# A decoder layer on one core: late weight blocks are loaded only after the last raw load of their projection

## The chip, the cores and the metric

The kernel runs on one core of one Trainium2 chip. The metric is the device time of one execution in microseconds; lower is better.

## The reference

One layer of a hybrid decoder over 256 positions of width 2048, in float32: a gated feed-forward network (FFN) at half weight, a mixer of attention and mLSTM heads behind one input projection and before one output projection, a second FFN, and a last norm.

```python
x = x + 0.5 * swiglu(rmsnorm(x, ffn1_norm), w_gate1, w_up1, w_down1)   # 2048 -> 5632 -> 2048
h = rmsnorm(x, mix_norm)
parts = split(h @ w_in)                                                # 2048 -> 6152
y = concat(diff_attention(...), mlstm(...))
x = x + y @ w_out                                                      # 2048 -> 2048
x = x + 0.5 * swiglu(rmsnorm(x, ffn2_norm), w_gate2, w_up2, w_down2)
out = rmsnorm(x, final_norm)
```

Nearly all of the work is in the projections (`@`). Each weight is used once, so all weights stream from HBM through the core: the profile counts 349.56 MB read.

## The kernel before, in words

**Splitting.** A float32 product is made of three matmuls in a faster format: each operand is split into a high and a low half (`split_weights`, L117 and L118 by way of `split`: ACT casts the high half `wh`, DVE subtracts it to make the low half `wl`), and `mms` (L166, L167, L169) adds high x high, low x high and high x low in PSUM. The pool `wsp` holds four pairs of `wh` and `wl`; ACT can only split the next weights when PE has used the oldest pair.

**Paired projections.** Two column blocks of 512 columns, from the weights `wa` and `wb` (gate and up of an FFN, or two neighbouring blocks), are computed together by the class `Paired`. For the first `ns` pairs of rows tiles (128 rows each) it uses a scheme with seven products instead of eight for a 2 x 2 block of weights (as Strassen's and Winograd's): sums of weight blocks take the place of a product. The other rows (`rest`) are multiplied plainly (`plain`, loads of `rawp` at L204). `ns` is 5 for most projections, 3 or 2 for the down projections and for a few of the mixer.

**The four blocks of a pair.** `load` (L430 and, through `load_pair`, L193) brings three of them into a tile `raw`: slot 0 is the first row tile of `wa`, slots 1 and 2 are both row tiles of `wb`. The fourth, the second row tile of `wa`, is called the late block. `late` (L495) loads late blocks two at a time into a tile `late` of the pool `wrp`, which has five buffers and serves the `rawp` tiles too. The `raw` tiles are in the pool `wr` with six buffers; a projection with `ns` = 5 takes five of them, so one is free for the projection that follows.

**Order within a projection.** `leading` loads the raw tiles, splits slot 0, and adds blocks on DVE (L463). `second_sum` then splits slot 0 again and adds slot 2 to it, with an accumulating DMA (L479, `raw<-raw`) where `ns` is over 3, or else on DVE. `sums` loads the late blocks, splits slot 0 once more (`part` with S2), adds the late blocks to slot 0 with accumulating DMAs (L517, `raw<-late`), multiplies the late blocks bare (`bare`), and goes on with slot 1. `second` uses slots 0 and 2, and frees the raw tiles. `Chain.run` runs the leading part of a projection between the last steps of the one before.

**Queues.** A scheduler orders each engine's instructions by their place in the program and by priorities; loads are moved forward by 400 places (`AHEAD`). SP's queue carries the `rawp` and `late` loads of all projections. The raw loads go on POOL's queue (`nc.gpsimd`), with the accumulating DMAs, except in the first chains of both FFNs (`ON_POOL` = 3), where they go on SP's too. A queue issues in order: where one issue waits, all behind it on that engine wait.

Of the kernel before, what the change touches and what calls it, by code (L numbers as in the profile page):

```python
# [42 lines left out]
LK = 4  # L43
# [17 lines left out]
def tile_trunk_layer(ctx: ExitStack, tc: tile.TileContext, x, xt, par, bias_if, lamv, fnorm,  # L61
                     wg1, wu1, wd1, wqk0, wqk1, wqk2, win, wout, wg2, wu2, wd2, out):
    nc = tc.nc
# [14 lines left out]
    def nm(s):  # L78
        uid[0] += 1
        return f"{s}_{uid[0]}"  # L80
# [43 lines left out]
    def after(late, early):  # L124

        tc.add_manual_dep(late.ins, early.ins.name,
                          mybir.DependencyInfo(mybir.DependencyClass.NoSync, mybir.DependencyReason.DATA),
                          reason="order")

    def ahead_of_splits(i, ins, slack=SLACK):  # L130
        queued[i].append((len(splits) + slack, ins))

# [2 lines left out]
    def split_weights(src, hi, lo):  # L135
        made = split(src, hi, lo)
        for late, q, past in zip(made, queued, ahead):
            while q and len(splits) >= q[0][0]:
                past.append(q.pop(0)[1])
            del past[:-3]  # L140
            for early in past:
                after(late, early)
        return made
# [46 lines left out]
            f()  # L190

    def load_pair(dst, w, k, queue=nc.sync):
        queue.dma_start(dst, w[k // LK][:, k % LK:k % LK + 2, :])  # L193

    def load_unit(w, k, pieces=(UK,), spare=False):
        n = w.shape[3]
# [13 lines left out]
    def in_turn(load):  # L210
        for early in turns[-1:]:
            after(load, early)
        turns.append(load)
# [99 lines left out]
    def gained(src, gain):  # L313
        g = wk("xg")
        for i in range(2):
            ahead_of_splits(0, act.activation(g[:, i * S:(i + 1) * S], src[:, i, :], AF.Copy, scale=gain[:, i:i + 1]))
        return g.rearrange("p (a b) -> p a b", b=P)
# [16 lines left out]
    def add_part(acc, hb, c):  # L334

        t = wk("part")
        with soon():
            ahead_of_splits(0, nc.scalar.activation(t, acc, AF.Copy, scale=0.5))
        nc.gpsimd.dma_start(xres[:, hb, c * CW:(c + 1) * CW], t, accum_op=ALU.add)

    def add_half(acc, xs, scale):
        with soon():
            ahead_of_splits(1, nc.vector.scalar_tensor_tensor(xs, acc, scale, xs, op0=ALU.mult, op1=ALU.add))
# [62 lines left out]
    class Paired:  # L406
# [17 lines left out]
        def load(self, j):  # L424
            n, off = self.n, self.off
            raw = wr.tile([P, 3, n], F32, tag="raw", name=nm("raw"))
            self.raws.append(raw)
            k = self.k0 + 2 * j
            with tc.high_priority(offset=AHEAD):
                self.queue.dma_start(raw[:, 0, :], self.wa[k // LK][:, k % LK, :])  # L430
                load_pair(raw[:, 1:3, off:], self.wb, k, self.queue)
                if off:
                    nc.gpsimd.memset(raw[:, 1:3, 0:off], 0.0)

# [55 lines left out]
        def late(self, js):  # L490

            raw = wrp.tile([P, UK, self.n], F32, tag="rawp", name=nm("late"))
            k = self.k0 + 2 * js[0]
            with tc.high_priority(offset=AHEAD):
                nc.sync.dma_start(raw[:, 0:len(js), :], self.wa[k // LK][:, k % LK + 1:k % LK + 2 * len(js):2, :])  # L495
            return raw

        def bare(self, js, raw):
# [395 lines left out]
    late = {}  # L894
# [376 lines left out]
```

## Time and profile before

| | |
|---|---|
| median of 3 runs | 1761.58 us (1761.36 to 1761.77) |
| the profiled execution | 1761.59 us, of which 1759.9 us are the span of its instructions |
| PE, DVE, ACT, POOL busy | 99%, 92%, 72%, 25% of the span |
| granted TensorE clock | 0.998 |
| moved by DMA | 429.72 MB, mean 244 GB/s |
| `late` loads | 108, on SP |
| accumulations L517, L479 | 176 and 92, on POOL |

How to read it: PE is the matmul engine, PEld its weight loads, DVE, ACT and POOL the other engines, SP the queue that only issues DMAs. Rows name a line, an engine, an operation and the tiles (out<-in). The time from an issue to the landing of a DMA holds its wait for the 16 DMA engines that all queues share.

### The profile page before, as it was taken

What the parts mean: (1) busy time and instruction counts of PE and PEld (TensorE: products, weight loads), DVE (VectorE), ACT (ScalarE), POOL (GpSimd) and SP (SyncE); (2) the same over time, 40 slices, a digit from 0 to 9 for tenths busy, and PEclk for the clock granted to TensorE, in tenths of its full rate; (3) what the DMA queues carried; (4) which work ended last, traced back from release to release, by engine and by line L of the source; (5) the groups of instructions that cost most, each with busy time, mean ns of one, the idle gap of its engine ahead of it and who ended that gap; (6) DMA issues with size and microseconds to landing.
All of it is one profiled execution on the core that took longest, in us unless ns stands there. A gap on an engine that the chain in (4) does not pass through costs nothing.

```text
span 1759.9 us, 24446 instructions
## 1 busy us (share of the span) xinstructions
PE 1745.6 (99%) x7926; PEld 1439.5 (82%) x7926; DVE 1618.5 (92%) x2188; ACT 1270.2 (72%) x1949; POOL 434.9 (25%) x631
## 2 busy tenths in 40 slices
PE   9999999999999999999999999999999999999997
PEld 7788888888888888987888888888888888888886
DVE  6999999999999999897888999999999999999997
ACT  7676777777677768677687777776777777677765
POOL 0032332333233312022231001232332332223310
PEclk9999999999999999999999999999999999999999
DMA  9887998999799976587886677897998999799973
GB/s 362 259 244 223 247 272 267 244 293 259 228 252 265 260 262 198 181 235 215 240 233 204 185 219 214 247 286 227 246 265 274 240 285 266 234 245 274 255 248 114
DMA packets 155265, 429.72 MB, mean 244 GB/s; under 512 B 17632, under 2 KB 18944, under 8 KB 154880
## 3 DMA queue, kind: packets, MB, share of 16 engines
q0 software_dynamic: 76304, 196.66, 44.9%
q1 hardware_dynamic: 77680, 229.40, 38.3%
q10 hardware_dynamic: 1152, 2.09, 0.3%
q8 instruction: 62, 1.02, 0.2%
q14 instruction: 67, 0.55, 0.1%
HBM read 349.56 MB, written 2.10 MB: 200 GB/s over the span
## 4 chain that ended last, share of the span: by engine, by line
PE 98%; DMA 1%; ACT 0%; issue 0%; DVE 0%; POOLq 0%; POOL 0%; SPq 0%; ACTq 0%
PE acc L166 19%; PE acc L167 19%; PE acc L169 19%; PE accn L166 12%; PE accn L167 12%; PE accn L169 12%; PE tr L357 1%; DMA raw<-late 0%; PE tr L298 0%; PE sc L1063 0%; PE num L1014 0%; PE tr L1102 0%; PE tr L808 0%; DMA raw<-in_wg_dram 0%; PE rr L984 0%
## 5 line engine op out<-in xcount | busy, mean ns | idle before, releaser
L117 ACT CAST wh<-raw 128x512 fp32r<-128x512 f32 (+2 forms) x885 | 599.6, 708 | 198.4 <-PE acc L167 85.3
L118 DVE TENSOR_TENSOR wl<-raw,wh 128x512 fp32r<-128x512 f32 (+2 forms) x885 | 675.3, 792 | 53.6 <-ACT wh L117 46.4
L117 ACT CAST wh<-rawp 128x1024 fp32r<-128x1024 f32 (+3 forms) x308 | 317.9, 1035 | 112.9 <-PE acc L167 56.4
L118 DVE TENSOR_TENSOR wl<-rawp,wh 128x1024 fp32r<-128x1024 f32 (+3 forms) x308 | 367.0, 1196 | 32.3 <-ACT wh L117 30.3
L166 PE MATMUL acc<-wh,xs 128*128 128x512 f32 (+2 forms) x956 | 369.6, 387 | 0.5 <-ACT wh L117 0.5
L167 PE MATMUL acc<-wh,xs 128*128 128x512 f32 (+2 forms) x956 | 368.8, 386 | 0.0
L169 PE MATMUL acc<-wl,xs 128*128 128x512 f32 (+2 forms) x956 | 316.9, 387 | 0.0
L517 POOL DMA_DIRECT2D raw<-late x176 | 154.5, 1059 | 467.0 <-DVE wl L118 447.7
L166 PE MATMUL acc<-wh,xt 128*128 128x512 f32 (+2 forms) x564 | 218.3, 388 | 0.7 <-ACT wh L117 0.7
L167 PE MATMUL acc<-wh,xt 128*128 128x512 f32 (+2 forms) x564 | 217.3, 386 | 0.0
L166 PE MATMUL accn<-wh,xt 128*128 128x512 f32 (+1 forms) x552 | 215.4, 391 | 0.1
L167 PE MATMUL accn<-wh,xt 128*128 128x512 f32 (+1 forms) x552 | 214.7, 390 | 0.0
L463 DVE TENSOR_TENSOR raw<-raw 128x1024 f32<-128x1024 f32 x176 | 211.0, 1217 | 0.8
L166 PEld LDWEIGHTS acc<-wh,xs 128*128 128x128 f32 x956 | 179.5, 188 | 37.1 <-ACT wh L117 1.4
L167 PEld LDWEIGHTS acc<-wh,xs 128*128 128x128 f32 x956 | 179.6, 188 | 35.8
L169 PEld LDWEIGHTS acc<-wl,xs 128*128 128x128 f32 x956 | 178.3, 188 | 37.0 <-DVE wl L118 1.3
L166 PE MATMUL accn<-wh,xs 128*128 128x512 f32 (+1 forms) x408 | 163.6, 402 | 2.3 <-ACT accn L487 1.7
L167 PE MATMUL accn<-wh,xs 128*128 128x512 f32 (+1 forms) x408 | 159.1, 391 | 0.0
L169 PE MATMUL acc<-wl,xt 128*128 128x512 f32 (+2 forms) x564 | 157.2, 386 | 0.0
L169 PE MATMUL accn<-wl,xt 128*128 128x512 f32 (+1 forms) x552 | 154.7, 388 | 0.0
L479 POOL DMA_DIRECT2D raw<-raw x92 | 80.4, 927 | 284.3 <-DVE wl L118 240.3
L169 PE MATMUL accn<-wl,xs 128*128 128x512 f32 (+1 forms) x408 | 141.3, 389 | 0.0
(209 smaller groups left out, 2129.8 us busy)
## 6 DMA issues: line engine op xcount, KB each, us to landing
rawp<-in_wd_dram SPq DMA_DIRECT2D x88, 512.0 KB, 5.4
raw<-late POOLq DMA_DIRECT2D x174, 256.0 KB, 5.2
raw<-in_wu_dram POOLq DMA_DIRECT2D x80, 512.0 KB, 7.5
rawp<-in_wu_dram SPq DMA_DIRECT2D x73, 512.0 KB, 5.3
rawp<-in_wg_dram SPq DMA_DIRECT2D x69, 512.0 KB, 5.1
raw<-raw POOLq DMA_DIRECT2D x92, 256.0 KB, 4.2
raw<-in_wd_dram POOLq DMA_DIRECT2D x44, 512.0 KB, 8.7
late<-in_wg_dram SPq DMA_DIRECT2D x41, 512.0 KB, 8.8
```

The costliest lines, as they stand in the source:

```text
L117: return (nc.scalar.copy(hi, src), nc.vector.tensor_tensor(out=lo, in0=src, in1=hi.bitcast(F32), op=ALU.subtract))
L118: nc.vector.tensor_tensor(out=lo, in0=src, in1=hi.bitcast(F32), op=ALU.subtract))
L166: nc.tensor.matmul(acc, lh, rh, start=first, stop=False, skip_group_check=on)
L167: nc.tensor.matmul(acc, ll, rh, start=False, stop=False, skip_group_check=on)
L169: newest[:] = [nc.tensor.matmul(acc, lh, rl, start=False, stop=last, skip_group_check=on)]
L357: nc.tensor.transpose(tr[:, i, hb * P:(hb + 1) * P], hs[hb][:, k * P:(k + 1) * P], ident)
L463: nc.vector.tensor_tensor(out=raw[:, 0:2, :], in0=raw[:, 0:3:2, :], in1=raw[:, 1:2, :].to_broadcast([P, 2, n]), op=ALU.add)
L479: nc.gpsimd.dma_start(raw[:, 0, :], raw[:, 2, :], accum_op=ALU.add)
L517: nc.gpsimd.dma_start(self.raws[j][:, 0, :], lates[-1][1][:, i, :], accum_op=ALU.add)
```

## The change

The function `landed` makes an instruction wait until another one is done (`after`, which was there before, only sets their order). `load_pair` returns its DMA, `load` keeps the newest one of the projection, and `late` makes its load wait until that DMA has landed, unless the raw loads are on SP's own queue.

```diff
+    def landed(late, early):
+
+        tc.add_manual_dep(late.ins, early.ins.name,
+                          mybir.DependencyInfo(mybir.DependencyClass.Sync, mybir.DependencyReason.DATA),
+                          reason="order")
+
     def load_pair(dst, w, k, queue=nc.sync):
-        queue.dma_start(dst, w[k // LK][:, k % LK:k % LK + 2, :])
+        return queue.dma_start(dst, w[k // LK][:, k % LK:k % LK + 2, :])
...
-                load_pair(raw[:, 1:3, off:], self.wb, k, self.queue)
+                self.newest_load = load_pair(raw[:, 1:3, off:], self.wb, k, self.queue)
...
-                nc.sync.dma_start(raw[:, 0:len(js), :], self.wa[k // LK][:, k % LK + 1:k % LK + 2 * len(js):2, :])
+                load = nc.sync.dma_start(raw[:, 0:len(js), :],
+                                         self.wa[k // LK][:, k % LK + 1:k % LK + 2 * len(js):2, :])
+                if self.queue is not nc.sync:
+                    landed(load, self.newest_load)
```

All engines' instructions stand in the same order as before; only waits differ. The leading parts of all raw loads of a projection come before its `sums`, so the load waited for is the projection's last. On SP's queue, around the late loads at 222 us. Names carry the program's numbers here; DMAHW and DMASW are the semaphores of the DMAs that SP and POOL issue, eight of each used in turn, and DVE is DVE's count of finished instructions. Before:

```order
87 L204 DMA rawp_458_2285<-in_wu1_dram 128x1024 [waits DMAHW2_49,DVE_49]
88 L495 DMA late_462_2307<-in_wg1_dram 128x2x512 [waits DMAHW3_49,DVE_49]
89 L495 DMA late_465_2323<-in_wg1_dram 128x2x512 [waits DMAHW4_49,DVE_49]
90 L495 DMA late_470_2349<-in_wg1_dram 128x512 [waits DMAHW5_49,DVE_49]
91 L204 DMA rawp_485_2413<-in_wg1_dram 128x1024 [waits DMAHW6_49,DVE_49]
```

And changed (the lines of the file have moved by six):

```order
87 L210 DMA rawp_458_2285<-in_wu1_dram 128x1024 [waits DMAHW2_49,DVE_49]
88 L501 DMA late_462_2307<-in_wg1_dram 128x2x512 [waits DMAHW3_49,DMASW6_49,DVE_49]
89 L501 DMA late_465_2323<-in_wg1_dram 128x2x512 [waits DMAHW4_49,DVE_49]
90 L501 DMA late_470_2349<-in_wg1_dram 128x512 [waits DMAHW5_49,DVE_49]
91 L210 DMA rawp_485_2413<-in_wg1_dram 128x1024 [waits DMAHW6_49,DVE_49]
```

The first late load of the projection has the wait for DMASW6; those behind it have the same wait by standing behind it on the queue. On POOL's queue the same projection, before and changed alike but for the line numbers; before:

```order
70 L430 DMA raw_442_2201<-in_wg1_dram 128x512 [waits DMASW4_49,DVE_49]
71 L193 DMA raw_442_2201<-in_wu1_dram 128x1024
72 L430 DMA raw_450_2250<-in_wg1_dram 128x512 [waits DMASW5_49,DVE_49]
73 L193 DMA raw_450_2250<-in_wu1_dram 128x1024 [waits DMASW6_49]
74 L430 DMA raw_521_2575<-in_wd1_dram 128x512 [waits DMASW7_49,DVE_49]
75 L193 DMA raw_521_2575<-in_wd1_dram 128x1024 [waits DMASW0_49]
76 L479 DMA raw_434_2160<-raw_434_2160 128x512 [waits DMASW1_49,DVE_49]
77 L479 DMA raw_435_2163<-raw_435_2163 128x512 [waits DMASW2_49,DVE_49]
```

Row 73 is the last raw load of the projection, for which the late load of row 88 now waits. Rows 74 and 75 already belong to the projection that follows. In the whole program 40 late loads have the new wait, one for each projection whose raw loads are on POOL's queue.

## The prediction

> **What bounds the kernel now.** I read the page first, then the waits of PE and of ACT, then the order in time of the DMA issues around a few late loads. From the page:
>
> ```profile
> span 1759.9 us, 24446 instructions
> PE 1745.6 (99%) x7926; PEld 1439.5 (82%) x7926; DVE 1618.5 (92%) x2188; ACT 1270.2 (72%) x1949; POOL 434.9 (25%) x631
> DMA  9887998999799976587886677897998999799973
> PE 98%; DMA 1%; ACT 0%; issue 0%; DVE 0%; POOLq 0%; POOL 0%; SPq 0%; ACTq 0%
> ```
>
> PE is busy for 99% of the span and is 98% of the chain that ended last. The DMA engines are busy too, 0.7 to 0.9 of most slices, so the change moves transfers about in a resource that has little idle time, for an engine that waits for almost none of them. The waits of PE from 70 us to the end (ahead of 70 us stand only late loads that the change leaves alone), then four rows of the list of all waits, then who waited for the plain weight loads of L204:
>
> ```profile
> PE acc L166 <- ACT wh L117: 0.5, 1, 0.5
> ...
> ACT wh L117 <- PE acc L167: 159.0, 236, 2.1
> ACT wh L117 <- DMA raw<-raw: 6.5, 12, 0.8
> ACT wh L117 <- DMA raw<-in_wg_dram: 5.8, 5, 2.2
> ...
>   ACT wh L117: 1.6, 2
> ```
>
> Columns: who waited for whom, us in total, times, longest. After 70 us PE waits 0.5 us in all. ACT, which makes the high halves of the weights, waits 159.0 us in this row alone for PE to give buffers back: the splitting runs ahead of PE. For transfers of raw tiles it waits 12.3 us in the two rows below it, and PE does not feel it. For L204 loads ACT waited 1.6 us in the whole program.
>
> **The change, part by part.** Nothing moves on any engine; 40 late loads, the first of their projection on SP, get one more semaphore, that of the last raw load of the same projection on POOL's queue. A typical one, at 222 us (start, us, engine, line, what; SP, POOL, ACT; then each transfer's time to landing):
>
> ```profile
> 222.14 10.88 SPq L495 DMA_DIRECT2D late<-in_wg_dram  x3
> 238.50 12.76 SPq L204 DMA_DIRECT2D rawp<-in_wg_dram  x3
> ...
> 225.21 0.53 POOL L193 DMA_DIRECT2D raw<-in_wu_dram  x1
> 235.90 0.88 POOL L479 DMA_DIRECT2D raw<-raw  x1 [9.01 <-DVE wl L118]
> 245.52 3.51 POOL L517 DMA_DIRECT2D raw<-late  x4 [2.95 <-DVE wl L118]
> ...
> 246.47 1.05 ACT L117 CAST wh<-late 128x1024 fp32r<-128x1024 f32 x1
> ...
> L193 POOL DMA_DIRECT2D raw<-in_wu_dram x1: 530/530/530, 225.2 to 225.2; - x1
> DMA to landing us min/median/max: 9.3/9.3/9.3
> ...
> L495 SPq DMA_DIRECT2D late<-in_wg_dram x3: 333/546/546, 222.1 to 232.7; - x3
> DMA to landing us min/median/max: 5.3/9.2/9.3
> ```
>
> Step 1, the late load itself. The last raw load lands at 225.2 + 9.3 = 234.5, so the first late load moves from 222.1 to 234.5, 12.4 us later. With the same time to landing (9.2) it is there at 243.7. Its first user, the accumulation of L517, starts at 245.52 and was released by DVE, not by the load; ACT's cast of it starts at 246.47. So 1.8 us are left, and the cost is 0. The widest delay and one that is none, read the same way:
>
> ```profile
> 1402.53 10.68 SPq L495 DMA_DIRECT2D late<-in_wg_dram  x3
> 1425.71 3.51 POOL L517 DMA_DIRECT2D raw<-late  x4 [2.63 <-DVE wl L118]
> L193 POOL DMA_DIRECT2D raw<-in_wu_dram x1: 530/530/530, 1405.6 to 1405.6; - x1
> DMA to landing us min/median/max: 10.8/11.5/12.2
> ...
> 153.12 0.55 SPq L495 DMA_DIRECT2D late<-in_wd_dram  x1
> L193 POOL DMA_DIRECT2D raw<-in_wd_dram x1: 530/530/530, 124.3 to 124.3; - x1
> DMA to landing us min/median/max: 9.6/10.3/11.0
> ```
>
> At 1402.5 the last raw load lands at 1405.6 + 12.2 = 1417.8: 15.3 us of delay, and with 9.2 us more the late tile lands at 1427.0, 1.3 us after the accumulation would start. At 153.1 the raw tiles are in by 135.3, and the wait is already over. Going through all 40 like this, 28 are delayed, at most by those 15.3 us, and 12 are not. Nowhere but at 1402.5 does the old time to landing reach past the first use by more than half a microsecond, and there the lead of the splitting takes it up. How long that lead is, where it is shortest in a usual projection:
>
> ```profile
> 254.25 1.89 DVE L118 TENSOR_TENSOR wl<-raw,wh 128x512 fp32r<-128x512 f32 x3
> ...
> 257.93 0.39 PE L169 MATMUL acc<-wl,xs 128*128 128x512 f32 x1
> ```
>
> The third of these splits ends at 254.25 + 1.89 = 256.1, and PE uses it at 257.9: a lead of 1.8 us. Cost of step 1: 0, at most 1.3 us.
>
> Step 2, what stands behind the late load on SP. The other late loads of the projection follow 0.55 us apart (the length of one issue, 546 ns), so three are out by 236.2, before the L204 load of 238.5, which therefore does not move. Where the late load is followed at once by a plain load, that one moves too, by an estimate from the issue times 1 to 4 us. Who waits for these loads is ACT, with the 1.6 us above in the whole program, so they land with time to spare. Cost 0. The 40 extra waits are instructions on SP alone.
>
> Step 3, the raw loads. They no longer share the DMA engines with the late loads. At 222 us the stretch between moves 390 GB/s at full share (first row below), so the 1 MB of the first two late loads is 2.7 us of DMA time taken out of the way of the last raw tiles. What that can bring is bounded by what PE loses: the 0.5 us of waits, and about 0.45 us at each of two crowded places (next step), 1.4 us in all. DVE works without a break there (6.00 of 6 us), so earlier data start little sooner. I take -0.1 us. The Trainium skill, "DMA: Bandwidth & Descriptors", section "Queues, rings and completion order", says that each DMA engine goes round-robin, packet by packet, between the queue rows that have work; by it the raw loads would get up to twice the rate while the late loads are held, which is the same sign as this step. The tail of 9 to 12 us on the last raw load agrees that the two queues share.
>
> Step 4, where the moved bytes go. They now run beside the L479 accumulations, which ACT waits for. At 222 us the DMA share of the following stretch has room. The places without room are the two at the start of an FFN part (310 us and, alike, 1367 us):
>
> ```profile
> 228.00:234.00 6.00, 6.00 (x28) 4.98 (x27) 6.00 (x8) 4.55 (x8) 0.00 (x0) 1.00 1.02 390
> 234.00:240.00 6.00, 6.00 (x28) 4.97 (x27) 6.00 (x8) 3.23 (x5) 1.78 (x3) 1.00 0.88 244
> ...
> 308.00:314.00 6.00, 6.00 (x28) 4.86 (x27) 6.00 (x8) 4.85 (x7) 1.24 (x3) 1.00 0.56 138
> 314.00:320.00 6.00, 6.00 (x28) 4.95 (x28) 6.00 (x8) 4.54 (x8) 1.83 (x3) 1.00 0.97 293
> 320.00:326.00 6.00, 6.00 (x28) 4.99 (x27) 6.00 (x8) 1.98 (x4) 3.08 (x4) 1.00 1.08 294
> 326.00:332.00 6.00, 6.00 (x26) 4.31 (x26) 5.25 (x9) 4.36 (x7) 2.10 (x4) 1.00 0.93 173
> ...
> 310.14 4.93 SPq L495 DMA_DIRECT2D late<-in_wg_dram  x3
> L193 POOL DMA_DIRECT2D raw<-in_wu_dram x1: 561/561/561, 312.7 to 312.7; - x1
> DMA to landing us min/median/max: 5.3/6.1/6.9
> L479 POOL DMA_DIRECT2D raw<-raw x4: 853/856/857, 322.6 to 327.2; - x4
>   ACT wh L117: 1.3, 2
> DMA to landing us min/median/max: 5.1/5.5/5.9
> ```
>
> Columns of the first rows: stretch, its length, busy time (count) of PE, PEld, DVE, ACT, POOL, granted clock, DMA share, GB/s. PE starts 26 matmuls instead of 28 from 326 to 332: 2 x 6/28 = 0.43 us lost, so the lead is nil here, and ACT already waits 1.3 us for these accumulations. The first late loads go out at 310.1, in a stretch with a DMA share of 0.56. Changed, they wait until 312.7 + 6.9 = 319.6, and their 1.05 MB fall into a share of 1.08: at 294 GB/s 3.6 us of DMA time. Low end 0: the raw tiles now land sooner, and all 1.3 MB of late tiles need 4.5 us at that rate, so from 319.6 they are through by 324.1, while the accumulations start at 322.6 and run until 332. High end: all 3.6 us at both places, 7.2 us. I take 0.3 us at each, near the low end, since the overlap is about 1.5 us of 9 and two queues share it: +0.6.
>
> Sum against the profiled execution, 1761.59 us (1759.9 of span and 1.7 around it; it lies 0.01 over the median of the runs, 1761.58): 0 + 0 - 0.1 + 0.6 = +0.5, so 1762.1 us.
>
> **The rivals.** *Slower: the accumulations are crowded.* Step 4 at its high end: the late tiles' 1.05 MB delay the L479 transfers at 310 and 1367 us by the full 3.6 us each, ACT waits, and PE, without a lead, waits with it: 1761.6 + 7.2 = 1768.8 us. It decides from 1.8 us at each place (3.5 us in all); elsewhere the lead of 1.8 us protects. For it: a share of 1.08, and the 1.3 us of waits. Against it: the raw tiles on the same POOL queue are ahead sooner. The Trainium skill, in the same page's "Rules for kernel authors", says to issue a DMA early and wait for it late, so that its fixed cost is covered; the change does the opposite. By that rule the step costs something wherever the cover is short, which the rows above say is here at two places only.
>
> *Faster: the raw tiles were what held the splitting.* For it: ACT's 5.8 us of waits for raw loads, which should go. Against it: PE waits 0.5 us after 70 us. Even if all 5.8 us reached PE the time would be 1761.6 - 5.8 = 1755.8; by PE's own rows it cannot pass 1.4 us, 1760.2.
>
> *The wait changes nothing*, because it is over nearly everywhere as it is at 153 us: 1761.6. The 28 places read above speak against it.
>
> **How the numbers follow.** 0.2% of the time is 3.5 us, about what a measurement of this kernel can tell from no change. The forecast, an effect between -1.4 and +3.5 us, has 0.74; no effect at all 0.04, which is also within the bound; crowding beyond 3.5 us 0.17; a gain beyond 3.5 us 0.05. So faster 0.05, same 0.78, slower 0.17. The range begins at the bound of the gain, 1760.2, and ends at 1765.3, half of the crowding's full price; above it lies about 0.13, below it 0.05.
>
> **What the profile would show.** Step 1: L495 at 222 us starts at 232 to 235, and POOL's L517 near 245.5 is still released by DVE. If L517 is released by a late load, step 1 is wrong. Step 2: ACT still waits under 3 us for L204 loads. Step 3: the waits of ACT for raw loads shrink from 5.8 us, and raw loads take less than 9 us to land. Step 4: at 322 to 332 us L479 takes no more than 6.5 us to land, and PE starts 25 or more matmuls from 326 to 332. The prediction fails if ACT's waits for raw<-raw grow from 6.5 to over 15 us and PE's waits with them, or if PE begins to wait for casts of late or rawp tiles.

## The result, and the profile after

The changed kernel takes 1784.48 us (median of 6 runs, 1776.33 to 1791.90), the kernel before 1761.47 us beside it (6 runs, 1760.46 to 1761.77). The ratio is 1.013, with an interval of 1.011 to 1.016: slower by 23 us, where +0.5 was forecast. The profiled execution took 1784.54 us, so its trace can be read against the median. The runs of the changed kernel lie 16 us apart, those of the one before 1.3. All lines behind L129 have moved: L172 to L175 are the matmuls, L199 and L436 the raw loads, L210 the `rawp` loads, L485 the second sums, L501 the late loads, L526 their accumulation.

From the page of the changed kernel: span, busy times, DMA share, the chain that ended last, and the second sums' accumulations with their median time to landing; then the last row as it was before:

```profile
span 1782.8 us, 24446 instructions
PE 1755.4 (98%) x7926; PEld 1436.2 (81%) x7926; DVE 1618.2 (91%) x2188; ACT 1269.6 (71%) x1949; POOL 432.8 (24%) x631
DMA  9887998898899986577886678887997999798973
PE 81%; DMA 7%; issue 5%; DVE 4%; ACT 1%; POOL 1%; SPq 0%; POOLq 0%; DVEq 0%; ACTq 0%
raw<-raw POOLq DMA_DIRECT2D x92, 256.0 KB, 6.7
...
raw<-raw POOLq DMA_DIRECT2D x92, 256.0 KB, 4.2
```

PE was 98% of the chain and is 81%; DMA, DVE, POOL and issue now stand in it. The span grew by 22.9 us: 9.8 are a longer busy time of PE, 13.1 idle time. The number of matmuls is the same; where they start further apart their records overlap less, so the busy time grows too. The waits, then three of SP's:

```profile
ACT wh L117 <- PE acc L173: 152.7, 208, 2.5
ACT wh L117 <- DMA raw<-raw: 39.9, 44, 2.3
POOL raw L526 <- DMA raw<-raw: 22.8, 10, 4.4
PE acc L172 <- ACT wh L117: 9.7, 11, 1.8
ACT wh L117 <- DMA raw<-in_wg_dram: 2.9, 5, 1.1
...
SPq L501 <- DMA raw<-in_wu_dram: 228.2, 17, 17.2
SPq L501 <- DMA raw<-in_wd_dram: 76.8, 8, 11.1
SPq L501 <- DMA raw<-in_win_dram: 42.3, 4, 15.2
```

The added wait is there: by the last three rows 29 late loads wait 347 us in all, 28 of them by the change (a wait of 0.6 us ahead of 70 us was there before). What grew behind it is ACT's wait for the second sums, 6.5 us before and 39.9 now, and PE's for ACT's casts. Among the waits none of ACT is for a late tile, and two, of 1.4 us together, are for `rawp` tiles; L526 waits for no late tile either. The chain of cause is to be seen at 222 us, the example of the prediction (SP, two rows of POOL, ACT, PE; then the four accumulations with their times to landing, now and, in the last row, before):

```profile
234.73 1.85 SPq L501 DMA_DIRECT2D late<-in_wg_dram  x3
...
235.72 0.88 POOL L485 DMA_DIRECT2D raw<-raw  x1 [6.89 <-DVE wl L118]
246.07 0.85 POOL L526 DMA_DIRECT2D raw<-late  x1 [3.68 <-DMA raw<-raw]
...
250.86 0.62 ACT L117 CAST wh<-raw 128x512 fp32r<-128x512 f32 x1 [1.28 <-DMA raw<-raw]
...
251.53 0.50 PE L172 MATMUL acc<-wh,xs 128*128 128x512 f32 x1 [1.65 <-ACT wh L117]
...
L485 POOL DMA_DIRECT2D raw<-raw x4: 853/867/879, 235.7 to 241.5; - x4
DMA to landing us min/median/max: 8.6/9.0/9.4
...
DMA to landing us min/median/max: 3.3/4.1/4.6
```

The last raw load is in by 234.7, and the three late loads go out from 234.73 to 236.6. The first accumulation is issued 1 us behind the first of them and takes 8.6 us, the others up to 9.4; before, the same four took 3.3 to 4.6. ACT waits for the sums four times, then PE waits 1.65 us for ACT. The same pieces of the trace by DMA queue, q0 being POOL's and q1 SP's (packets, MB, share of the 16 engines): 237 to 240 us after, then 236 to 240 us before.

```profile
q1 hardware_dynamic: 350, 0.68, 88.0%
...
q0 software_dynamic: 257, 0.52, 71.3%
q1 hardware_dynamic: 105, 0.18, 11.6%
```

After, in three microseconds in which two accumulations stood issued (235.72 and 237.46), POOL's queue moved not one packet; SP's moved 350. In the kernel before, the first packet of the first accumulation came 1.5 us after its issue; now it came 4.9 us after it (the packets are matched to the issues by their sizes).

Matmul by matmul (PE's order is unchanged), PE falls behind in five-pair projections of the FFNs: 5.3 us between 200 and 300 us, 5.9 between 325 and 440, 2.9 between 1255 and 1358, 6.0 between 1383 and 1420, 4.7 between 1462 and 1685, 24.8 in all (the first 100 us were 1.9 us shorter, and 0.8 to 1.9 in every other run here). In the mixer, and where `ns` is 2 or 3, it loses nothing.

### The profile page after: what moved, and what is told of

It is laid out like the page before. It is cut to its first block, busy times and chain, and to the rows that moved or that the text cites. A ratio compares the mean times of both kernels' runs of the same rounds, so it can differ in the third digit from the quotient of the medians.

```text
span 1782.8 us, 24446 instructions
## 1 busy us (share of the span) xinstructions
PE 1755.4 (98%) x7926; PEld 1436.2 (81%) x7926; DVE 1618.2 (91%) x2188; ACT 1269.6 (71%) x1949; POOL 432.8 (24%) x631
## 2 busy tenths in 40 slices
DMA packets 155265, 429.72 MB, mean 241 GB/s; under 512 B 17632, under 2 KB 18944, under 8 KB 154880
## 4 chain that ended last, share of the span: by engine, by line
PE 81%; DMA 7%; issue 5%; DVE 4%; ACT 1%; POOL 1%; SPq 0%; POOLq 0%; DVEq 0%; ACTq 0%
PE acc L172 15%; PE acc L173 15%; PE acc L175 15%; PE accn L175 11%; PE accn L172 11%; PE accn L173 11%; DMA raw<-raw 4%; DVE wl L118 3%; ACT wh L117 1%; PE tr L363 1%; DMA raw<-in_wu_dram 1%; POOL raw L485 1%; DMA raw<-late 1%; DMA late<-in_wd_dram 1%; PE tr L304 0%
## 5 line engine op out<-in xcount | busy, mean ns | idle before, releaser
L172 PE MATMUL acc<-wh,xs 128*128 128x512 f32 (+2 forms) x956 | 371.5, 389 | 9.2 <-ACT wh L117 9.0
L175 PE MATMUL acc<-wl,xs 128*128 128x512 f32 (+2 forms) x956 | 318.6, 388 | 0.3
L526 POOL DMA_DIRECT2D raw<-late x176 | 153.3, 980 | 504.3 <-DVE wl L118 459.1
L172 PEld LDWEIGHTS acc<-wh,xs 128*128 128x128 f32 x956 | 179.7, 188 | 50.6 <-ACT wh L117 15.6
L172 PE MATMUL acc<-wh,xt 128*128 128x512 f32 (+2 forms) x564 | 218.3, 388 | 0.7 <-ACT wh L117 0.7
L172 PE MATMUL accn<-wh,xt 128*128 128x512 f32 (+1 forms) x552 | 215.3, 391 | 0.1
L175 PEld LDWEIGHTS acc<-wl,xs 128*128 128x128 f32 x956 | 178.4, 188 | 42.1 <-DVE wl L118 6.7
L172 PE MATMUL accn<-wh,xs 128*128 128x512 f32 (+1 forms) x408 | 163.2, 401 | 2.5 <-ACT wh L117 1.7
L175 PE MATMUL acc<-wl,xt 128*128 128x512 f32 (+2 forms) x564 | 157.2, 386 | 0.0
L175 PE MATMUL accn<-wl,xt 128*128 128x512 f32 (+1 forms) x552 | 154.7, 388 | 0.0
L485 POOL DMA_DIRECT2D raw<-raw x92 | 80.3, 925 | 281.1 <-DVE wl L118 245.2
L175 PE MATMUL accn<-wl,xs 128*128 128x512 f32 (+1 forms) x408 | 142.6, 392 | 2.7 <-DVE wl L118 2.7
```

Source lines behind the costliest of these rows:

```text
L172: nc.tensor.matmul(acc, lh, rh, start=first, stop=False, skip_group_check=on)
L175: newest[:] = [nc.tensor.matmul(acc, lh, rl, start=False, stop=last, skip_group_check=on)]
L485: nc.gpsimd.dma_start(raw[:, 0, :], raw[:, 2, :], accum_op=ALU.add)
L526: nc.gpsimd.dma_start(self.raws[j][:, 0, :], lates[-1][1][:, i, :], accum_op=ALU.add)
```

## The experiments

The theories, by the names used below. *A*: the held late tiles, up to 1.28 MB released at once, stand ahead of the accumulations `raw<-raw` in the DMA engines; these land late, then ACT, then PE. Later A is split: *A1* says that the bytes issued just ahead do it, *A2* that the DMA engines' idle time between the last raw load's landing and the first late packet does it (their share at 234 to 240 us fell from 0.88 to 0.65). *B*: SP's queue is held, so that plain loads behind the late ones come late. *C*: the late tiles themselves come late.

**Where the loss is: five-pair projections only, small ones only.** Each diff is against the changed kernel.

```diff
-                if self.queue is not nc.sync:
+                if self.queue is not nc.sync and self.ns > 3:
```

> The wait stays only where five pairs of a projection run by the seven-product scheme (ns over 3), the projections whose sums use the accumulating DMA raw<-raw. Theory A (the held late tiles, 1.3 MB in one burst, stand ahead of raw<-raw in the DMA engines): all of the loss stays, 1778 to 1790 us, ACT waits 30 us or more for raw<-raw, and raw<-raw takes about 6.5 us to land instead of 4.2. Rival B (SP's queue is held, so the plain loads behind the late ones come late in every delayed projection): 19 of 28 delayed projections are left, so about two thirds of the 23 us: 1776 us, and ACT waits for rawp tiles. Rival C (the late tiles themselves are late): as A in time, but ACT waits for late tiles and raw<-late is released by a late load.

```diff
-                if self.queue is not nc.sync:
+                if self.queue is not nc.sync and self.ns <= 3:
```

> The wait stays only where two or three pairs run by the scheme, where no raw<-raw DMA is made and 9 late loads are delayed by 3 to 9 us. A: 1761.5 us within 1 us of before. B: a third of the loss stays, 1769 us. C: some loss, 1764 to 1769 us, with ACT waiting for late tiles.

The first took 1782.15 us (ratio 1.0126, 1.0098 to 1.0154), the second 1761.17 (0.9999, 0.9989 to 1.0009). Within the intervals the whole loss (21 of the 23 us) comes from the projections with `ns` over 3, the only ones with accumulations `raw<-raw` by DMA. In the small ones SP is held too, 88 us in nine waits, and it costs nothing, which speaks against B.

**Release by an earlier raw load.** The raw loads are kept in a list; the late loads wait for the last but one (first version) or, with five pairs, the last but two (second).

```diff
-            self.raws = []
+            self.raws, self.loads = [], []
...
-                self.newest_load = load_pair(raw[:, 1:3, off:], self.wb, k, self.queue)
+                self.loads.append(load_pair(raw[:, 1:3, off:], self.wb, k, self.queue))
...
-                    landed(load, self.newest_load)
+                    landed(load, self.loads[-2])
```

> All waits stay, but for the last raw load but one; in the profile of before that one lands about 2.5 us sooner (231.9 against 234.5 us at the projection of 222 us). A: the late burst is 2.5 us further through when raw<-raw is issued, so raw<-raw lands after about 5 us and most of the loss goes: 1763 to 1770 us. B and C: the delay falls from 12.4 to 10 us, so the loss shrinks by a fifth: 1780 us.

```diff
+                    landed(load, self.loads[-3 if self.ns > 2 else -2])
```

> All waits stay, for the last raw load but two (of five), which lands about 6 us sooner (228.6 against 234.5 us). A: the late tiles are through before raw<-raw is issued: 1761 to 1764 us, raw<-raw lands after 4 to 4.6 us. B and C: the delay is half of what it was, so half of the loss: 1773 us.

They took 1762.04 us (1.0004, 0.9995 to 1.0014) and 1761.00 (1.0000, 0.9991 to 1.0009). The same 1.28 MB are still held back, but at 222 us they are released some 5 us sooner. That costs less than A expected of the first. In that version SP still waits 237 us in 23 added waits, so B and C, which expected most of the loss to stay, fail here. At 222 us, with the last but one (SP, POOL, the four accumulations):

```profile
229.55 2.69 SPq L501 DMA_DIRECT2D late<-in_wg_dram  x3
...
235.13 0.88 POOL L485 DMA_DIRECT2D raw<-raw  x1 [9.01 <-DVE wl L118]
...
DMA to landing us min/median/max: 3.6/4.1/4.6
```

Released at 229.55, the late tiles are nearly through when the accumulations come: their last packet starts at 237.1, the first accumulation's first at 236.6, and the accumulations land as before. It is not the holding that costs, but what is released just ahead of the accumulations.

**How much is released.** Five-pair projections only; of the three late loads only the third (256 KB) waits, or the second and the third (768 KB).

```diff
+                if self.queue is not nc.sync and self.ns > 3 and js is self.twos[-1]:
```

> Of the three late loads of a five-pair projection only the third (256 KB) waits for the last raw load; the first two (1 MB) go out early, as before. Theory A1, the held bytes are served ahead of the second sums' accumulations raw<-raw because they are issued just ahead of them: the delay goes with the bytes released there. All 1.28 MB raise the median landing of raw<-raw from 4.2 to 6.6 us, so 0.26 MB raise it by about 0.5, to 4.7; no transfer reaches the 7.8 us from which PE lost time; 1761 to 1763 us. Theory A2, it is the DMA engines' idle time between the last raw load's landing and the first late packet: with the first two late loads out early nothing idles; 1761 to 1762. A theory in which a late tile that waits is itself missed: the third tile is the one with the most time left; 1761.

```diff
+                if self.queue is not nc.sync and self.ns > 3 and js is not self.twos[0]:
```

> The second and third late loads (768 KB of 1.28 MB) of a five-pair projection wait for the last raw load, the first (512 KB) goes out early. Theory A1 (bytes released just ahead of the accumulations): raw<-raw lands at a median of 4.2 + 2.4 x 0.6 = 5.6 us, the crowded places pass 7.8 us, and a part of the 21 us is lost, 1764 to 1775 us. Theory A2 (idle time of the DMA engines before the burst): the first late load's 512 KB are out early and cover a part of the idle time, but the raw loads end at the same time, so the idle time is the same as with all three held, and the loss is about as large, 1775 to 1785, or nothing if those 512 KB fill it, 1761 to 1763.

| released by the last raw load | time, us | ratio | `raw<-raw`, median us | ACT's waits for it, us |
|---|---|---|---|---|
| nothing (small projections only) | 1761.17 | 0.9999 (0.9989 to 1.0009) | 4.3 | 6.4 |
| 256 KB | 1763.26 | 1.0011 (1.0001 to 1.0020) | 4.5 | 12.4 |
| 768 KB | 1769.56 | 1.0045 (1.0030 to 1.0060) | 6.2 | 24.3 |
| 1280 KB (five-pair only) | 1782.15 | 1.0126 (1.0098 to 1.0154) | 6.6 | 36.4 |

The loss goes with the bytes released. Against A1's numbers the time with 256 KB is 0.3 us over the range, one of its accumulations took 8.2 us where none was to reach 7.8, and the landing with 768 KB is 0.6 us over the estimate; the rest is within. A2's two outcomes for 768 KB, 1775 or more and 1763 or less, both missed. At 222 us, the four accumulations' landing with 256 KB, then with 768 KB:

```profile
DMA to landing us min/median/max: 3.3/4.1/4.6
...
DMA to landing us min/median/max: 6.4/6.6/7.9
```

**The bytes without the tiles.** All late loads go out early. Behind each, a second load of the same bytes goes into one spare buffer that nobody reads; it waits for the last raw load, or is free. The diff leaves out the pools: the spare buffer is new, and the work pool is made smaller to hold it.

```diff
+                    twin = spare.tile([P, UK, self.n], F32, tag="twin", name=nm("twin"))
+                    load = nc.sync.dma_start(twin[:, 0:len(js), :],
+                                             self.wa[k // LK][:, k % LK + 1:k % LK + 2 * len(js):2, :])
+                    landed(load, self.newest_load)
```

> All late loads go out early as in the kernel before. Each of a five-pair projection is followed by a second load of the same bytes into one spare buffer that nobody reads, and this one waits for the last raw load (the spare buffer makes each wait for the one before it too, so at most 512 KB stand in line at a time; the work pool has five buffers instead of seven to make room). About 30 MB more are moved. Theory A1: the extra bytes stand ahead of raw<-raw though no used load was moved at all; raw<-raw lands 1 to 2 us later than in the version with free twins, and the time is 3 to 15 us longer than that one's. Theory A2 (idle time left by the held loads): no used load leaves a gap, so the time is within 2 us of that of the free twins. A theory in which held late tiles are themselves missed: likewise no difference.

> The same extra loads into the spare buffer, but free: each goes out with its late load, at the early time. It is the measure for the held twins. All theories: 30 MB more in DMA engines that are 0.7 to 1.0 busy in the FFN stages; 1761 to 1770 us, with raw<-raw at 4.2 to 5 us.

The held twins took 1790.31 us, the free ones 1855.33, and the comparison failed. With no wait to hold them, the scheduler moved the free twins of the whole program far forward, in front of loads of the first 300 us that are used; PE lost some 88 of its 96 us there. In the held version some late loads stood behind a held twin on SP and so were held too. Neither isolates the bytes. Only 19 of the 23 five-pair projections have their raw loads on POOL's queue, so the twins moved 24.9 MB more (by the pages, 454.62 MB for 429.72), not about 30.

A second pair mends the order: two extra loads (768 KB) only behind the third late load, each tied behind the load ahead of it with `after`. All engines have the same order in both versions.

```diff
+                if self.queue is not nc.sync and self.ns > 3 and js is self.twos[-1]:
+                    twin = spare.tile([P, 3, self.n], F32, tag="twin", name=nm("twin"))
+                    for i in range(0, 3, 2):
+                        m, early = min(2, 3 - i), load
+                        k = self.k0 + 2 * i
+                        load = nc.sync.dma_start(twin[:, i:i + m, :],
+                                                 self.wa[k // LK][:, k % LK + 1:k % LK + 2 * m:2, :])
+                        after(load, early)
+                        landed(load, self.newest_load)   # only where held
```

> The late loads of the five-pair projections go out early as before; behind the third one stand two extra loads (768 KB, bytes already loaded, into a spare buffer that nobody reads), and these wait for the last raw load. The work pool has four buffers instead of seven to make room. The order on every engine is that of the version with free extra loads, the measure for this one. Theory A1 (whatever is issued just ahead of the accumulations is served first): raw<-raw lands at a median of 5.5 to 6.5 us as with 768 KB of late tiles held, and the time is 4 to 12 us over that of the free extra loads, though no load that is used was moved. Theory A2 (the loss needs the idle gap that held late loads leave): no more than 2 us over it. Theory that held late tiles are themselves missed: no difference.

> The same two extra loads, behind the third late load on SP, but free: they go out some 12 us earlier, beside the raw loads. 17.7 MB more are moved (23 projections by 768 KB). All theories: 1761 to 1772 us, with raw<-raw at 4.2 to 5 us.

Held: 1792.69 us (1.0181, 1.0164 to 1.0198), `raw<-raw` at 6.8 us, 0.3 over A1's range. Free: 1781.51 (1.0117, 1.0102 to 1.0132), at 6.1 us; the time is 10 us over its range. Both moved 15.0 MB more (444.67 for 429.72), 19 projections by 768 KB, and not 17.7. The reason for the free version's miss stands in SP's rows at 222 us, free first, each with its accumulations; the last two rows are the DMA share (last but one column) of the free and of the held version from 234 to 240 us:

```profile
223.89 10.40 SPq L502 DMA_DIRECT2D late<-in_wg_dram  x3
234.35 1.18 SPq L509 DMA_DIRECT2D twin<-in_wg_dram  x2
...
DMA to landing us min/median/max: 5.7/6.2/7.2
...
236.89 1.19 SPq L509 DMA_DIRECT2D twin<-in_wg_dram  x2
...
DMA to landing us min/median/max: 4.9/7.4/8.1
...
234.00:240.00 6.00, 6.00 (x28) 4.95 (x28) 6.00 (x8) 3.78 (x6) 1.76 (x2) 1.00 1.04 387
234.00:240.00 6.00, 6.00 (x28) 4.99 (x27) 6.00 (x8) 3.45 (x6) 2.27 (x3) 1.00 0.82 221
```

The free extra loads were not early: they stand behind the third late load, which waits for its buffer until 234, so they too came just ahead of the accumulations (here from 237.2). In the free version no load waits for the last raw load at all, the DMA engines have no gap (1.04), and the accumulations are late even so: A2 is not needed for it. Between the two versions the bytes and the order are the same and only the moment of the release differs, by 2.5 us here; the held ones cost 11.2 us more, within A1's 4 to 12. But the held version has a gap here too (0.82), so these 11.2 us do not tell the moment from the gap. How much of the free version's 20 us is the moment, how much the 15.0 MB more that the DMA engines carry, and how much the work pool of four buffers, these runs do not separate.

**Late loads behind the first accumulation.** Now they wait until the first of the four accumulations has landed; order on all engines as before.

```diff
+                        ins = nc.gpsimd.dma_start(raw[:, 0, :], raw[:, 2, :], accum_op=ALU.add)
+                        if j == 0:
+                            self.first_sum = ins
...
+                if self.queue is not nc.sync and self.by_dma:
+                    landed(load, self.first_sum)
```

> The late loads of the five-pair projections wait for the landing of the first of the four accumulations raw<-raw instead of the last raw load: they go out still later (by some 6 us at 222 us), but the second and third accumulations are already issued then. Order on all engines as before. Theory A1, DMAs on different queues are served nearly in order of issue: the accumulations that were issued before the late loads land as before, a median of 4.2 to 5 us and no group at 8; instead the late tiles come up to 6 us late, ACT and POOL wait for late tiles (over 10 us in all, where it was none), and the time is 1765 to 1830 us. Theory S, the DMA engines share among the queues, so that any 1.28 MB beside the accumulations slow those in flight: raw<-raw at 5.5 to 7 us again, with the late tiles late on top of it, 1785 us or more.

It took 1825.79 us (1.0367, 1.0349 to 1.0386). At 222 us, on SP and on POOL; then the time to landing of the first, second, third and fourth accumulation, each by itself; then the packets of all loads and accumulations from 243 to 245 us, SP's alone:

```profile
241.27 1.86 SPq L503 DMA_DIRECT2D late<-in_wg_dram  x3
...
237.89 0.88 POOL L485 DMA_DIRECT2D raw<-raw  x1 [7.75 <-DVE wl L118]
239.62 0.87 POOL L485 DMA_DIRECT2D raw<-raw  x1 [0.85 <-DVE wl L118]
241.96 0.85 POOL L485 DMA_DIRECT2D raw<-raw  x1 [1.47 <-DVE wl L118]
243.70 0.85 POOL L485 DMA_DIRECT2D raw<-raw  x1 [0.88 <-DVE wl L118]
...
DMA to landing us min/median/max: 3.3/3.3/3.3
...
DMA to landing us min/median/max: 3.8/3.8/3.8
...
DMA to landing us min/median/max: 7.9/7.9/7.9
...
DMA to landing us min/median/max: 8.8/8.8/8.8
...
q1 hardware_dynamic: 186, 0.37, 97.3%
```

The two accumulations issued ahead of the late loads land in 3.3 and 3.8 us. They do not decide between A1 and S: the second still stood issued when the late loads went out at 241.27, but its packets were through at 242.5, and the first packet of a late load came at 242.6. The third decides. It was issued 0.7 us behind the first late load and takes 7.9 us; from 243 to 245 us, 1.0 to 3.0 us after its issue, POOL's queue moved no packet and SP's moved 186. Over all 23 projections the medians by place in the group are 3.3, 3.8, 7.9 and 8.8 us (before: 3.6, 4.5, 4.2, 4.3). That is nearly service by the order of issue, A1, and not equal sharing, S; the time by itself would have fitted both. A1's waits for late tiles came (POOL waits 14.2 us for them). Its miss: two, not three, had gone out, so the third and fourth were late after all, in a group at 8 us that was not to be, with ACT's waits for `raw<-raw` at 74 us.

## Why the prediction was wrong

**Step 1 (the late load itself, cost 0) held.** The late loads at 222 us start at 234.73, within 232 to 235, 28 late loads are delayed as the step counted, and no row of ACT waits for a late tile. The sign that was to show it, POOL's L526 still released by DVE, failed: it starts at 246.07, released by `raw<-raw`, as the rows at 222 us show. It was late, but not by the late load.

**Step 2 (what stands behind it on SP, cost 0) held.** SP was held 347 us, and ACT got no new wait for `rawp` loads; the run with small projections only agrees.

**Step 3 (raw loads sooner) held in part, and brought nothing.** ACT's waits for raw loads of `in_wg` fell from 5.8 to 2.9 us, and the raw loads of `in_wu` on POOL's queue have a median of 6.9 us to landing, 7.5 before. At the step's own example the last raw load took 9.2 us, 9.3 before, and not less than 9; so its tail, which the step took for a sign that the two queues share, is there without late loads beside it too. PE had nothing to gain from it.

**Step 4 (where the moved bytes go) failed.** It was priced at +0.3 us at two places; it cost 23 us in the FFNs' five-pair projections. Three parts of it were wrong.

- *"Two queues share it."* The step took the overlap of 1.5 us for the price since both queues would move along. The runs show the order of issue: 4.9 us to the first packet with late loads issued ahead, and, in the last experiment, 3.8 and 7.9 us for two neighbours of one group with the late loads issued between them. The Trainium skill, "DMA: Bandwidth & Descriptors", section "Queues, rings and completion order", has each DMA engine go round-robin between the queue rows, packet by packet. By that an accumulation of 256 KB would be through when about twice its bytes had moved, 0.5 MB, which at the 251 GB/s of 246 to 252 us is an estimate of 2 us, or 3.5 with the 1.5 us to the first packet; it took 8.6, and in three of these microseconds no packet of its queue moved at all. The trace disagrees, unless POOL's queue had nothing ready for the DMA engines in that time, which the trace does not show.
- *"At 222 us the DMA share of the following stretch has room."* The share there, 0.88, was that of the moved bytes at their old place too. Held, they leave a gap ahead and come as one block behind it. The windows of the changed kernel, and in the last row the last of them before (last but one column the DMA share; the count in the first brackets is PE's):

```profile
228.00:234.00 6.00, 6.00 (x28) 4.95 (x28) 6.00 (x8) 4.65 (x8) 0.53 (x1) 1.00 0.96 380
234.00:240.00 6.00, 6.00 (x28) 4.99 (x27) 6.00 (x8) 3.04 (x5) 1.96 (x3) 1.00 0.65 182
240.00:246.00 6.00, 6.00 (x29) 4.95 (x28) 4.48 (x6) 2.87 (x4) 1.51 (x2) 1.00 1.06 256
246.00:252.00 6.00, 4.35 (x19) 3.13 (x18) 1.87 (x3) 2.87 (x5) 2.56 (x3) 1.00 1.11 251
...
246.00:252.00 6.00, 6.00 (x28) 4.98 (x27) 5.83 (x8) 4.04 (x7) 3.90 (x5) 1.00 1.04 213
```

  A mean share over 6 us does not tell which transfer goes first.
- *"Elsewhere the lead of 1.8 us protects."* It does against 1.8 us. The accumulations at 222 us took 3.9 to 5.4 us longer each (8.6 to 9.4 for 3.3 to 4.6), and POOL's following accumulations stood behind them on its queue. So PE started 19 matmuls instead of 28 from 246 to 252 us, at a place that the step had left out.

At one of the two places that the step had named, 322 us, it looked as follows (three of the accumulations, ACT's waits for them, then two windows):

```profile
L485 POOL DMA_DIRECT2D raw<-raw x3: 851/853/855, 326.0 to 329.0; - x3
  ACT wh L117: 3.2, 3
DMA to landing us min/median/max: 7.9/8.0/8.2
...
326.00:332.00 6.00, 6.00 (x27) 4.44 (x25) 5.25 (x8) 2.93 (x5) 3.41 (x4) 1.00 1.07 282
332.00:338.00 6.00, 5.24 (x20) 3.45 (x21) 4.03 (x6) 2.40 (x5) 1.51 (x2) 1.00 1.11 248
```

8.0 us instead of at most 6.5. The 25 matmuls from 326 to 332 us were there (27), since the loss came one stretch later: 20 from 332 to 338 us, 28 before. By then the program ran 3.5 us late, so its stretches are not quite those of before.

The rival "the accumulations are crowded" had the mechanism, and the sign of failure (ACT's waits for `raw<-raw` over 15 us, PE's with them) came as written. Its price, 7.2 us, was that of two places; in 14 of the 19 five-pair projections whose late loads are held, the median of the four accumulations grew by 1 us or more. The rule of the Trainium skill that the prediction names beside it, to issue a DMA early and wait for it late, had the right sign, but the loss came by another way: the late loads themselves were not missed.

(The range's upper end was half of the rival's full price, 1761.6 + 3.6 = 1765.2, put down as 1765.3.)

What is not shown: why the runs of the changed kernel spread over 16 us. A late accumulation delays POOL's next raw loads, and these the next release, which would carry a small difference on; that was argued from the order on POOL's queue and not tried. Nor was a version tried in which the held tiles go out with the accumulations taken off the DMA engines.

## What to carry to other kernels

When a transfer is held back until another has landed, ask which short transfers are issued in the first microseconds after the release, since they will stand behind it: price the release as if all released bytes go first, not as a share. Read the time to landing of the short transfers that an engine waits for, not the mean DMA share; at 222 us the former doubled where the share of the next stretch fell. And a release only a few microseconds sooner (here one raw load sooner) can make the same wait free.

## What the runs showed of the hardware

- DMAs of SP and POOL were served nearly in the order of their issue across the two queues where a burst on SP was issued about 1 us ahead: the 3 us without a packet of POOL's queue and the run behind the first accumulation show it. The order is not strict: in the version with free extra loads POOL's queue moved 196 packets and SP's 236 from 239 to 242 us, most of SP's from loads issued ahead of the accumulations. Which part of the hardware sets this order, and whether POOL's transfers were ready any sooner, stays open.
- An accumulating packet is slow: in the packet records of the kernel before, the median is 178 ns for packets of 2 KB on POOL's queue, nearly all of them from accumulations, and 84 ns for those on SP's queue, from late loads. In the released burst, 237 to 240 us, the late loads' median is the same 84 ns but the mean 126, so some packets there took far longer.
- Over all 1104 accumulations of twelve traces (all here but that of the free twins), the median time to landing was 4.0 us where less than 300 KB of loads issued on SP had not landed at the issue, 4.6 with 300 to 600 KB, 6.1 with 600 to 900 KB, and 7.9 with 900 to 1200 KB. It grows no further: 7.2 with 1200 to 1500 KB and 8.0 above.
